# Side steps paced by the transposes' banks, the gates of the two branches apart, the conv weights loaded ahead, and the last 128 features by halves of tokens

## The chip, the core and the metric

One core of a Trainium2 chip. The metric is device time in microseconds (us) of one execution of the whole step, as the median of the runs shown. TensorE is called PE in the rows, VectorE DVE, ScalarE ACT, GpSimd POOL and SyncE SP.

## The reference

A step of a decoder trunk of two layers, all in fp32, for a prompt of 512 tokens and 8 sample tokens that share the weights. For each layer, on tokens x of 1024 features:

```python
xn = rmsnorm(x, g_mix)
u_a, v_a, q, k, v, gate_a, gate_b = split(xn @ w_in)      # 512, 512, 3 x 768, 2 x 1024 columns
a_out = gelu(u_a) * (tril(w_s) @ rmsnorm(gelu(v_a), g_v) + b_s)   # chunks of 128 tokens, 8 groups
b_out = merge of 3 dilated window attentions over q, k, v  # QK norm, rotary, softmax; 12 heads of 64
merged = sigmoid(gate_a) * (a_out @ w_a_proj) + sigmoid(gate_b) * (b_out @ w_b_proj)
x = x + merged @ w_o
up = rmsnorm(x, g_ffn) @ w_up                              # 2 x 2816 columns
c = conv_b + sum(conv_w[j] * up[t - 2 + j] for j in range(3))     # causal, along tokens
x = x + (silu(c_gate) * c_val) @ w_down
```

The sample tokens attend to cached keys and values, and their convolution starts from a cached state (`state_conv`). Outputs are the tokens after both layers, new key and value rows, conv rows and gating rows.

## The kernel before

Features lie on the 128 partitions, the 520 tokens along the free dimension in two halves of 260. Each weight block of 128 x 128 is split into a rounded part `hi` and a rest `lo` (ACT casts, DVE subtracts), and so are the activations; a block is then worth three products (hi x hi, hi x lo, lo x hi), for each half of the tokens: `triple` issues these six matmuls, all at line L362. Some tiles of the feed-forward use seven products in place of eight (`dense2`). PSUM has five banks for accumulation (`acc`) and three for everything else on PE (`tp`, from `tps()`): the transposes, the attention's scores and products, the gating products.

The order of the work is written out as a list of weight groups, whose raw blocks SP loads ahead in a ring of nine. `dense` runs a group: it takes the blocks, issues the triples, and hands the two banks of each 128 output features to a `unit` function, which reads them out at a raised priority. In each layer come the q, k and v columns of the three attentions with the u and v columns between, then the mix stage in the order of the string `mix`, then `w_o`, then the feed-forward with the up tiles and, piece by piece, the down projection. In `mix`, `gi` is a pair of features' worth of gate a (`gates`, 96 matmuls), `hi` one of gate b, `aj` 128 features of `a_out @ w_a_proj` (24 matmuls, read out by `gated`, L1378), `bj` 128 features of `b_out @ w_b_proj` (12 matmuls), added to `aj`'s and split for `w_o`.

Everything else is in generators ("side steps"): the attention blocks, the gating branch `a_branch`, the samples' attention `attn_samples`, the norms, `history` (the conv state's share), `conv_rows`, and `y_rows`, which transposes the last output back and stores it. They stand in lanes and are advanced by `pump`, which every triple calls. A planned clock `st["now"]` grows by 0.36 us for a triple into one bank and by 0.72 into two. A generator yields how long it wants to wait (times 1.1); a positive value says that its next step is heavy, a negative one that it is light. Heavy steps take 0.4 planned us each and may only follow one another at a distance (`GAP`). `finish` drains lanes at once: `a0` is preceded by `finish("v")` (the gating branch), `b0` by `finish("a", "s")` (attention and samples), the norm before the feed-forward by `finish("v")` (history). The order of emission gives each instruction its priority; a scheduler that runs when the program is built orders each engine's queue by it, and the engines run their queues in order.

`conv_columns` is the first part of `history` in layer 0: it brings the conv weights of both layers into columns (`cwc`), by a load of rows and a transpose for each of the three taps. In the last `into_x` of layer 1 (m = 7) 128 output features are accumulated in two banks that are filled in turn and added to `x`; `ready` counts the features that are done, and `y_rows` waits on it, for features 0 to 3, 4 to 6 and 7.

Of the kernel before, what the change touches and what calls it, by code (L numbers as in the profile page):

```python
# [22 lines left out]
H2 = 260  # L23
# [59 lines left out]
DELAY0 = 1.0  # L83
GAP = 0.7
SLACK = 1.1
# [4 lines left out]
def step_kernel(ctx: ExitStack, tc: tile.TileContext, a, o):  # L90
# [68 lines left out]

    mix = "g0 g1 g2 a0 a1 g3 a2 a3 h0 a4 a5 h1 h2 b0 a6 b1 b2 a7 b3 h3 b4 b5 b6 b7".split()  # L160
    for l in range(DEPTH):
# [65 lines left out]
    for g, grp in enumerate(groups):  # L227
# [10 lines left out]
        for k, k1 in steps(nk):  # L238
# [3 lines left out]
    raws, splits, parts4 = [], {}, {}  # L242
    st = {"raw": 0, "taken": 0, "split": 0, "used": set(), "g": 0, "now": 0.0, "last": -9.0,
          "pin": False, "limit": 0}
# [81 lines left out]
    def pump(force=()):  # L326

        while True:
            e = [q + [n] for n, k in LANES.items() if not force or n in force for q in tasks[n][:k]]
            if not force:  # L330
                e = [q for q in e if q[0] <= st["now"] and (q[2] or st["now"] >= st["last"] + GAP)]
            if not e:
                return
            due, g, light, n = min(e, key=lambda q: q[0])
            st["now"] = max(st["now"], due)
            lane = tasks[n]
            i = next(i for i, q in enumerate(lane) if q[1] is g)
            if not light:
                st["now"] += 0.4
                st["last"] = st["now"]  # L340
            try:
                d = next(g)
                lane[i][0] = st["now"] + SLACK * abs(d)
                lane[i][2] = d < 0
            except StopIteration:
                lane.pop(i)
            if force:
                return
# [262 lines left out]

    def conv_columns():
        for j in range(3):
            cr = tmp(128)
            for l in range(DEPTH):
                dma(cr[l * 44 : l * 44 + 44], a["conv_w"][l, j].rearrange("(m p) -> m p", p=128))
            yield 4.0
            t = tps()
            pe.transpose(t[:, :88], cr[:88], ident[:88, :88])
            dve.tensor_copy(cwc[:, j], t[:, :88])  # L620


# [48 lines left out]
    def y_rows():  # L671
        for k0, k1 in ((0, 4), (4, 7), (7, 8)):
# [3 lines left out]
            yield 1.3  # L676
            if n == 128:
                t = tps()
                for b in range(4):
                    pe.transpose(t[:, b * 128 : b * 128 + 128], x[:, k0, b * 128 : b * 128 + 128], ident)  # L680
                y = tmp(512).rearrange("p (b m) -> p b m", b=4)
                dve.tensor_copy(y, t.rearrange("p (b m) -> p b m", b=4))  # L682
                dma(o["yp"][0, :, k0 * 128 :].rearrange("(b p) m -> p b m", p=128), y)
            for b in range(4) if n > 128 else ():
# [12 lines left out]
            act.copy(ys[:, k0 * 128 : k1 * 128], t[:NB, :n])  # L697
        dma(o["ys"][:, 0], ys)


    for l in range(DEPTH):
# [681 lines left out]
        for g, j in mix:  # L1383
# [3 lines left out]
            elif g == "a":  # L1387
                if j == 0:
                    finish("v")
                    add("v", history())  # L1390
                gated(m1[j], As)
            else:
                if j == 0:
                    finish("a", "s")
                g = gb[j]
                gated(g, Bx)
                dve.tensor_tensor(g, g, m1[j], op=ALU.add)
                mgs.append((tmp(T, F32R), tmp(T, F32R)))
                split_f(*mgs[j], g)
# [93 lines left out]
        def down(g):  # L1493
            return [hs[k] for k in range(*pieces[g])]

        for op, i, *m in ffn:
            if op == "up":
# [10 lines left out]
        for m in (0, 2, 3, 4, 5, 6, 7):  # L1508
            into_x(m, down(3), 1.0, norm, last)
        if norm:  # L1510
# [40 lines left out]
```

## Time and profile before

| | |
|---|---|
| median of 3 runs | 1578.58 us (1576.14 to 1580.62) |
| profiled execution | 1577.19 us, of which the span from first to last instruction is 1575.2 us |
| PE busy | 1537.3 us, 98% |
| DVE busy | 1195.7 us, 76% |
| ACT busy | 781.1 us, 50% |
| POOL busy | 196.3 us, 12% |
| mean granted clock of PE | 0.994 |

A row of a group of instructions gives line, engine, operation, what is written and read, its count, and the time. Matmuls overlap in the records, so one that lasts 280 ns is followed by the next after some 120 ns; waits and stretches tell more of PE than its busy time.

### The profile page before, as it was taken

The page shows a single profiled execution, that of the slowest core. Times are in us where ns is not written, and L with a number is a line of the kernel's source. Part 1 is how long each engine was busy: PE and PEld are TensorE (multiplying, and loading weights), DVE is VectorE, ACT ScalarE, POOL GpSimd, SP SyncE. Part 2 cuts the span into 40 slices and gives each one's busy share as a digit, 9 for nine tenths or more (in the row PEclk, how much of TensorE's full clock was granted, in tenths as well). Part 3 has the DMA queues.
Part 4 walks back from the last instruction along what each step waited for, and adds up shares of the span by engine and source line. Part 5 has one row for each costly group of instructions (what it writes and reads, how often), then busy time and mean ns, then how long its engine had stood idle before and what let it go on. Part 6 is the DMA issues. An engine that isn't in the chain of part 4 may idle for free. (4 is left out here: it accounts for less than half of the span.)

```text
span 1575.2 us, 33158 instructions
## 1 busy us (share of the span) xinstructions
PE 1537.3 (98%) x12745; PEld 1508.1 (96%) x12745; DVE 1195.7 (76%) x2507; ACT 781.1 (50%) x1676; POOL 196.3 (12%) x138
## 2 busy tenths in 40 slices
PE   7999999999999999899999999999999999999998
PEld 7999899999999999899999998999999999999998
DVE  5677868866588898888848686878566979988793
ACT  6564535434354554555545554553344555545452
POOL 1112010000000132133002030100000003322210
PEclk9999999999999999999999999999999999999999
DMA  7443333533322323332444333334332223342331
GB/s 208 139 119 114 96 114 95 163 88 109 88 74 80 109 85 105 91 98 87 115 120 127 100 123 88 111 106 149 93 103 84 72 85 101 91 117 78 98 89 66
DMA packets 298301, 164.38 MB, mean 104 GB/s; under 512 B 18599, under 2 KB 291767, under 8 KB 298127
## 3 DMA queue, kind: packets, MB, share of 16 engines
q1 hardware_dynamic: 298143, 162.26, 35.3%
q8 instruction: 101, 1.65, 0.4%
q14 instruction: 57, 0.47, 0.1%
HBM read 154.66 MB, written 10.36 MB: 105 GB/s over the span
## 5 line engine op out<-in xcount | busy, mean ns | idle before, releaser
L362 PE MATMUL acc<-t,whi 128*128 128x260 f32 x7584 | 1306.1, 286 | 18.2 <-ACT t L465 7.6
L362 PEld LDWEIGHTS acc<-t,whi 128*128 128x128 f32 x7584 | 1094.7, 189 | 26.7 <-ACT t L465 9.2
L362 PE MATMUL acc<-t,wlo 128*128 128x260 f32 x3792 | 880.0, 285 | 0.0
L362 PEld LDWEIGHTS acc<-t,wlo 128*128 128x128 f32 x3792 | 633.9, 189 | 2.4 <-issue 0.7
L298 ACT CAST whi<-raw 128x512 fp32r<-128x512 f32 (+2 forms) x518 | 299.1, 579 | 481.8 <-PE acc L362 348.1
L299 DVE TENSOR_TENSOR wlo<-raw,whi 128x512 fp32r<-128x512 f32 (+2 forms) x518 | 351.7, 680 | 119.8 <-ACT whi L298 116.3
L1432 DVE SCALAR_TENSOR_TENSOR t<-t,cwc,t 128x510 f32<-128x510 f32 (+1 forms) x176 | 146.1, 841 | 22.0 <-ACT t L1430 21.8
L281 POOL TENSOR_TENSOR sum<-raw,raw 128x512 f32<-128x512 f32 x40 | 61.3, 1532 | 485.2 <-DMA raw<-in_w_up_dram 328.7
L138 POOL TENSOR_TENSOR rr<-ss,mhalf 128x8 f32<-128x8 f32 (+1 forms) x30 | 56.2, 1872 | 287.9 <-DVE ss L801 212.7
L1124 DVE TENSOR_TENSOR t<-acc,t 128x260 f32<-128x260 f32 x144 | 54.7, 419 | 34.9 <-PE acc L362 34.9
L298 ACT CAST whi<-sum 128x512 fp32r<-128x512 f32 x80 | 49.6, 620 | 61.2 <-PE acc L362 61.1
L609 ACT CAST t<-t 128x520 fp32r<-128x520 f32 (+1 forms) x84 | 47.2, 563 | 54.7 <-DVE t L1449 31.6
L1407 DVE TENSOR_TENSOR x<-acc,x 128x260 f32<-128x260 f32 x128 | 48.8, 419 | 31.8 <-PE acc L362 31.1
L1430 ACT ACTIVATE t<-t,vcol,cwc 128x520 f32<-128x520 f32 x88 | 72.1, 820 | 0.0
L299 DVE TENSOR_TENSOR wlo<-sum,whi 128x512 fp32r<-128x512 f32 x80 | 58.7, 737 | 16.8 <-ACT whi L298 16.6
L610 DVE TENSOR_TENSOR t<-t,t 128x520 fp32r<-128x520 f32 (+1 forms) x84 | 53.9, 644 | 12.5 <-ACT t L609 11.2
L138 POOL TENSOR_TENSOR rc<-ms,mhalf 128x5 f32<-128x5 f32 x4 | 4.7, 1177 | 430.9 <-DVE ms L515 430.9
L457 DVE TENSOR_TENSOR t<-acc,t 128x260 f32<-128x260 f32 x100 | 41.6, 423 | 7.4 <-PE acc L362 5.4
L911 ACT ACTIVATE t<-t,stat 128x128 f32<-128x128 f32 (+1 forms) x96 | 40.0, 419 | 7.7 <-DVE stat L908 7.3
L1189 DVE TENSOR_TENSOR t<-acc,t 128x260 f32<-128x260 f32 x76 | 29.2, 421 | 16.8 <-PE acc L362 14.9
L1448 ACT ACTIVATE t<-t 128x520 f32<-128x520 f32 x44 | 28.0, 637 | 24.1 <-DVE t L1432 15.1
L281 POOL TENSOR_TENSOR sum<-sum,raw 128x512 f32<-128x512 f32 x20 | 32.7, 1635 | 19.9 <-issue 19.0
(202 smaller groups left out, 1259.1 us busy)
## 6 DMA issues: line engine op xcount, KB each, us to landing
raw<-in_w_up_dram SPq DMA_DIRECT2D x176, 256.0 KB
raw<-in_w_in_dram SPq DMA_DIRECT2D x162, 256.0 KB
raw<-in_w_down_dram SPq DMA_DIRECT2D x96, 192.0 KB
t<-in_cache_kv_w_dram SPq DMA_DIRECT2D x48, 256.0 KB
raw<-in_w_o_dram SPq DMA_DIRECT2D x32, 256.0 KB
raw<-in_w_a_proj_dram SPq DMA_DIRECT2D x16, 256.0 KB
raw<-in_w_down_dram SPq DMA_DIRECT2D x32, 128.0 KB
out_dram<-t SPq DMA_DIRECT2D x15, 256.0 KB
```

What stands on the lines that cost most here:

```text
L138: pool.tensor_tensor(out, in_, mhalf[: in_.shape[0], :n], op=ALU.pow)
L281: pool.tensor_tensor(s, p, q, op=op)
L298: kept(act.copy(hi[:, :nk], r))
L299: kept(dve.tensor_tensor(lo[:, :nk], r, hi[:, :nk].bitcast(F32), op=ALU.subtract))
L362: mm = pe.matmul(b, wi, xi[:, h * H2 : h * H2 + H2], start=start and i == 0, stop=stop and i == 2,)
L457: return lambda acc: dve.tensor_tensor(out, acc, p, op=ALU.add)
L609: act.copy(hi, src)
L610: dve.tensor_tensor(lo, src, hi.bitcast(F32), op=ALU.subtract)
L1124: dve.tensor_tensor(v2(g)[:, h], acc, n.rb[:, h], op=ALU.mult)
L1407: dve.tensor_tensor(xm, acc, xm, op=ALU.add)
L1430: act.activation(cv, up, AF.Identity, scale=cwc[:, 2, i : i + 1], bias=vcol[:, 32 + i : 33 + i])
L1432: dve.scalar_tensor_tensor(cv[:, s:TP], up[:, : TP - s], cwc[:, j, i : i + 1], cv[:, s:TP], op0=ALU.mult, op1=ALU.add)
```

## The change

Four edits. `pump` no longer asks for a distance between heavy steps; it holds three slots, each taken by a heavy step for 3.0 planned us, and lets a heavy step go when one is free. In `mix` all groups of gate a and the `a` stand ahead of those of gate b and the `b`, except that `b0` to `b2` begin among the `h`; `history` is added after `a7` instead of before `a0`. `conv_columns` issues its six loads in a first step, waits 8.0, and then transposes the three in steps of their own. The last 128 features of the last layer are accumulated one half of the tokens after the other (`last_rows`), each added to `x` when it is done; `y_rows` transposes and stores each half by itself, the first by ACT, the second by DVE; and the sample rows' store is issued by ACT's queue instead of SP's.

```diff
--- before.py
+++ after.py
@@ -81,7 +81,7 @@
 
 SEVEN = tuple(("up", i) for i in (9,10,12,13,15,16,18,19,20,21))
 DELAY0 = 1.0
-GAP = 0.7
+BUSY = 3.0
 SLACK = 1.1
 URGENT = 60
 
@@ -157,7 +157,7 @@
             if 0 <= i - i0 < 3:
                 ffn.extend(("down", g, sum(ns[: i - i0]) + j) for j in range(ns[i - i0]))
 
-    mix = "g0 g1 g2 a0 a1 g3 a2 a3 h0 a4 a5 h1 h2 b0 a6 b1 b2 a7 b3 h3 b4 b5 b6 b7".split()
+    mix = "g0 g1 a0 a1 g2 a2 a3 g3 a4 a5 a6 a7 h0 h1 b0 h2 b1 b2 h3 b3 b4 b5 b6 b7".split()
     for l in range(DEPTH):
         w_in = a["w_in"][l]
 
@@ -240,7 +240,7 @@
                 loads.append((w, k0 + k, k1 - k, c))
                 blocks.append((g, (k, c)))
     raws, splits, parts4 = [], {}, {}
-    st = {"raw": 0, "taken": 0, "split": 0, "used": set(), "g": 0, "now": 0.0, "last": -9.0,
+    st = {"raw": 0, "taken": 0, "split": 0, "used": set(), "g": 0, "now": 0.0, "free": [0.0] * 3,
           "pin": False, "limit": 0}
     at = {b: i for i, b in enumerate(blocks)}
 
@@ -328,7 +328,7 @@
         while True:
             e = [q + [n] for n, k in LANES.items() if not force or n in force for q in tasks[n][:k]]
             if not force:
-                e = [q for q in e if q[0] <= st["now"] and (q[2] or st["now"] >= st["last"] + GAP)]
+                e = [q for q in e if q[0] <= st["now"] and (q[2] or st["now"] >= min(st["free"]))]
             if not e:
                 return
             due, g, light, n = min(e, key=lambda q: q[0])
@@ -337,7 +337,8 @@
             i = next(i for i, q in enumerate(lane) if q[1] is g)
             if not light:
                 st["now"] += 0.4
-                st["last"] = st["now"]
+                st["free"].remove(min(st["free"]))
+                st["free"].append(st["now"] + BUSY)
             try:
                 d = next(g)
                 lane[i][0] = st["now"] + SLACK * abs(d)
@@ -610,14 +611,16 @@
         dve.tensor_tensor(lo, src, hi.bitcast(F32), op=ALU.subtract)
 
     def conv_columns():
+        rows = [tmp(128) for _ in range(3)]
         for j in range(3):
-            cr = tmp(128)
             for l in range(DEPTH):
-                dma(cr[l * 44 : l * 44 + 44], a["conv_w"][l, j].rearrange("(m p) -> m p", p=128))
-            yield 4.0
+                dma(rows[j][l * 44 : l * 44 + 44], a["conv_w"][l, j].rearrange("(m p) -> m p", p=128))
+        yield 8.0
+        for j in range(3):
             t = tps()
-            pe.transpose(t[:, :88], cr[:88], ident[:88, :88])
+            pe.transpose(t[:, :88], rows[j][:88], ident[:88, :88])
             dve.tensor_copy(cwc[:, j], t[:, :88])
+            yield 1.0
 
 
     x = cp.tile([128, 8, T], F32, name="x")
@@ -674,13 +677,19 @@
             while ready[0] < k1:
                 yield -0.7
             yield 1.3
-            if n == 128:
+            for h in range(2) if n == 128 else ():
+                while ready[0] < k1 + h:
+                    yield -0.5
                 t = tps()
-                for b in range(4):
-                    pe.transpose(t[:, b * 128 : b * 128 + 128], x[:, k0, b * 128 : b * 128 + 128], ident)
-                y = tmp(512).rearrange("p (b m) -> p b m", b=4)
-                dve.tensor_copy(y, t.rearrange("p (b m) -> p b m", b=4))
-                dma(o["yp"][0, :, k0 * 128 :].rearrange("(b p) m -> p b m", p=128), y)
+                for b in range(2):
+                    c = h * 256 + b * 128
+                    pe.transpose(t[:, b * 128 : b * 128 + 128], x[:, k0, c : c + 128], ident)
+                y = tmp(256).rearrange("p (b m) -> p b m", b=2)
+                with urgent():
+                    (act.copy if h == 0 else dve.tensor_copy)(y, t[:, :256].rearrange("p (b m) -> p b m", b=2))
+                dma(
+                    o["yp"][0, h * 256 : h * 256 + 256, k0 * 128 :].rearrange("(b p) m -> p b m", p=128), y
+                )
             for b in range(4) if n > 128 else ():
                 t = tps()
                 for k in range(k0, k1):
@@ -695,7 +704,7 @@
                 j = (k - k0) * 128
                 pe.transpose(t[:NB, j : j + 128], x[:, k, TP:], ident)
             act.copy(ys[:, k0 * 128 : k1 * 128], t[:NB, :n])
-        dma(o["ys"][:, 0], ys)
+        act.dma_start(o["ys"][:, 0], ys)
 
 
     for l in range(DEPTH):
@@ -1387,8 +1396,9 @@
             elif g == "a":
                 if j == 0:
                     finish("v")
+                gated(m1[j], As)
+                if j == 7:
                     add("v", history())
-                gated(m1[j], As)
             else:
                 if j == 0:
                     finish("a", "s")
@@ -1493,6 +1503,23 @@
         def down(g):
             return [hs[k] for k in range(*pieces[g])]
 
+        def last_rows(xs):
+
+            g = st["g"]
+            st["g"] += 1
+            _, _, _, nk, (c,) = groups[g]
+            held = [(k0, k1, block(g, (k0, c))) for k0, k1 in steps(nk)]
+            for h in range(2):
+                acc = acc_tile()
+                for k0, k1, (hi, lo) in held:
+                    for k in range(k0, k1):
+                        xk = [t[:, h * H2 : h * H2 + H2] for t in xs[k]]
+                        triple((hi[:, k - k0], lo[:, k - k0]), xk, [acc], k == 0, k == nk - 1)
+                xm = v2(x[:, 7])[:, h]
+                with urgent():
+                    dve.tensor_tensor(xm, acc, xm, op=ALU.add)
+                ready[0] += 1
+
         for op, i, *m in ffn:
             if op == "up":
                 h_tile(i)
@@ -1506,7 +1533,10 @@
         else:
             norm = Norm(l * 8 + 8)
         for m in (0, 2, 3, 4, 5, 6, 7):
-            into_x(m, down(3), 1.0, norm, last)
+            if last and m == 7:
+                last_rows(down(3))
+            else:
+                into_x(m, down(3), 1.0, norm, last)
         if norm:
             norm.finish()
         finish("v", "s")
```

## Rows read from the trace of the kernel before

**Rows 1.** The page, engines: busy us, share of the span, instructions.
```profile
PE 1537.3 (98%) x12745; PEld 1508.1 (96%) x12745; DVE 1195.7 (76%) x2507; ACT 781.1 (50%) x1676; POOL 196.3 (12%) x138
```

**Rows 2.** Waits of PE: us in total, times, longest us.
```profile
PE tp L619 <- DMA t<-in_conv_w_dram: 2.3, 1, 2.3
PE acc L362 <- DVE t L1378: 2.1, 1, 2.1
...
PE tp L926 <- ACT t L928: 1.9, 2, 1.0
```

**Rows 3.** Timeline, layer 0: start us, us, engine, line, operation.
```profile
289.17 0.80 SPq L616 DMA_DIRECT2D t<-in_conv_w_dram  x2
...
293.27 0.38 PE L619 MATMUL tp<-cst,t 88*128 88x88 f32 x1 [2.33 <-DMA t<-in_conv_w_dram]
```

**Rows 4.** Windows after two waits: from:to, us, engines busy, clock, DMA share, GB/s.
```profile
293.25:296.65 3.40, 3.38 (x16) 3.40 (x17) 3.40 (x10) 0.61 (x2) 0.00 (x0) 0.50 0.97 291
296.65:300.00 3.35, 3.35 (x31) 3.35 (x31) 3.35 (x10) 1.40 (x5) 0.00 (x0) 1.00 1.02 322
...
1068.05:1071.47 3.42, 3.42 (x18) 3.42 (x17) 3.42 (x11) 1.85 (x4) 0.00 (x0) 0.50 1.01 339
1071.47:1076.00 4.53, 4.53 (x40) 4.53 (x39) 4.53 (x13) 1.42 (x3) 0.00 (x0) 1.00 0.62 197
```

**Rows 5.** Windows of the transposes' clusters (PE, PEld, DVE, ACT, POOL; clock).
```profile
188.27:193.34 5.07, 3.22 (x31) 2.03 (x30) 3.84 (x10) 3.50 (x14) 0.00 (x0) 1.00 0.23 48
193.34:200.00 6.66, 6.66 (x56) 6.66 (x57) 3.30 (x8) 2.88 (x8) 0.00 (x0) 1.00 0.32 81
...
960.70:965.65 4.95, 3.09 (x30) 1.95 (x29) 3.46 (x10) 3.51 (x14) 0.00 (x0) 1.00 0.17 46
965.65:969.10 3.45, 3.45 (x19) 3.40 (x16) 1.33 (x4) 1.48 (x5) 0.00 (x0) 0.51 0.08 5
969.10:975.00 5.90, 5.90 (x52) 5.90 (x51) 2.51 (x4) 1.41 (x4) 0.00 (x0) 1.00 0.31 89
```

**Rows 6.** Line 1108, the samples' last transposes: ns min/median/max, first and last start.
```profile
L1108 PE MATMUL tp<-cst,t x8: 170/256/256, 327.5 to 1100.6; 128*128 128x8 f32 x8
```

**Rows 7.** Timeline, layer 0, DVE: the gating branch's last product.
```profile
190.26 0.69 DVE L1307 SCALAR_TENSOR_TENSOR t<-t,t 128x520 f32<-128x520 f32 x1
```

**Rows 8.** Windows of the cache burst in both layers (third column DVE).
```profile
289.00:299.60 10.60, 8.27 (x59) 8.06 (x58) 10.60 (x31) 2.39 (x6) 0.00 (x0) 0.84 1.01 318
...
1063.70:1073.60 9.90, 7.85 (x55) 7.68 (x54) 9.90 (x29) 2.86 (x6) 0.00 (x0) 0.83 1.00 327
```

**Rows 9.** Groups of DVE from 289 to 317: count, busy us, mean ns, idle before.
```profile
L299 DVE TENSOR_TENSOR wlo<-raw,whi 128x512 fp32r<-128x512 f32 x8 | 5.4, 681 | 0.0
...
L1378 DVE SCALAR_TENSOR_TENSOR t<-t,acc 128x260 f32<-128x260 f32 x6 | 2.4, 416 | 0.3 <-PE acc L362 0.3
...
L1335 DVE TENSOR_TENSOR t<-t,cwc 128x176 f32<-128x176 f32 x4 | 1.2, 330 | 0.0
...
L1341 DVE TENSOR_TENSOR hc<-t 128x176 f32<-128x176 f32 x2 | 0.7, 330 | 0.0
```

**Rows 10.** Timeline of the end.
```profile
1569.06 0.41 PE L362 MATMUL acc<-t,wlo 128*128 128x260 f32 x2
...
1569.38 0.76 DVE L1407 TENSOR_TENSOR x<-acc,x 128x260 f32<-128x260 f32 x2 [4.56 <-PE acc L362]
...
1570.67 0.69 DVE L682 COPY t<-tp 128x512 f32<-128x512 f32 x1 [0.53 <-PE tp L680]
1571.06 0.30 SPq L698 DMA_DIRECT2D out_dram<-ys  x1
1571.77 0.38 SPq L683 DMA_DIRECT2D out_dram<-t  x1
```

**Rows 11.** Window of the last store's data (last columns DMA share, GB/s).
```profile
1572.50:1573.75 1.25, 0.00 (x0) 0.00 (x0) 0.00 (x0) 0.00 (x0) 0.00 (x0) 0.79 0.68 216
```

**Rows 12.** Waits of SP's queue: us in total, times, longest us.
```profile
SPq L265 <- DVE wlo L299: 777.1, 349, 8.1
```

## The prediction

> **What bounds the kernel now.** I read the engine totals first. TensorE (PE) is busy 1537.3 of 1575.2 us, VectorE (DVE) 76% [rows 1], so PE is the bound and only what stops or slows PE can be won: at most some 38 us of idle time and what the clock costs. Next the waits of PE, longest total first [rows 2]. Three kinds lie in stages that the diff touches: one wait of 2.3 us for the load of the conv weights, one of 2.1 us for DVE's `gated` (L1378), and short ones of the attention's transposes on ScalarE (ACT) copies.
>
> The timeline shows the first: the third pair of conv loads is issued at 289.17, in the middle of a burst of cache loads, and the transpose of L619 that needs it starts at 293.27 after 2.33 us of waiting [rows 3]. PE runs its queue in order, so the accumulations behind it stand too. The windows show the second half of the price: after that wait the granted clock is 0.50 (1.2 instead of 2.4 GHz) from 293.25 to 296.65, and 16 PE instructions take 3.40 us where the next stretch does 31 in 3.35 [rows 4]. The same happens in layer 1 after the wait for `gated`: 18 instructions in 3.42 us, then 40 in 4.53. Without transposes between, an accumulation matmul costs 6.66 / 56 = 0.119 us [rows 5]; I use it as PE's price.
>
> **The change, part by part.**
>
> *Conv weights.* Six loads before the first transpose instead of two before each: no work is added but one more `yield`. The first transpose is due 8 x 1.1 = 8.8 us after the issues. The loads need three times 0.80 us of SP issue plus gaps, some 3 us, and the last pair took 4.1 us from issue to its use, in a stretch of saturated DMA [rows 3]; 7.1 is less than 8.8. They also move from ahead of `a0` to behind `a7`, past the cache burst. Gain: 2.33 us of wait and 3.40 - 16 x 3.35 / 31 = 1.67 us of half clock, **4.0 us**. Bounds: 0 (the loads come late again) to 4.0; I take 4.0, for the one thing that was late has 1.7 us to spare. Six issues in a row on SP hold raw loads up by some 3 us; the raw ring runs five blocks of 2.9 us ahead, which hides it. The three tiles held instead of one come out of 61. Next late after this wait are the outputs of `gated` in the full DVE of that stretch, below. POOL's queue is passed by nothing.
>
> *Order of the mix stage.* The same groups in another order. Counting 48 matmuls to a feature of a gate, 24 to an `a`, the groups ahead of `b0` are 816 matmuls before and 768 after, so `b0` comes 48 x 0.119 = 5.7 us earlier. `b0` forces the attention and the samples to their end; the samples' last transposes run at 327.5 in layer 0 and `b0` stood, by count, at 340.6 [rows 6], so some 7 us of margin stay and this costs nothing; with the margin gone it would cost the excess. `a0` comes 11.5 us earlier; the gating branch that it waits for ran its last L1307 at 190.26 in layer 0 [rows 7], long before either place, so nothing there.
>
> The place to watch is the cache burst. From 289.0 to 299.6 DVE is busy 10.60 of 10.60 us and in layer 1 from 1063.7 to 1073.6 9.90 of 9.90 [rows 8]: it adds up the sampled V rows. There PE waited for `gated`. In the new order `a4` to `a7`, four in a row, lie about there. Their DVE work is 8 x 0.416 for the outputs and 4 x 0.68 for the weights, 6.0 us in 11.4; two features' worth of gate `h0` takes 4 x 0.416 + 4 x 0.68 = 4.4 [rows 9]. So 1.6 us more DVE where it is full; `history` leaving the same stretch takes away 1.2 us of L1335 and some 0.7 of the add behind it. About even. But five accumulation banks, two to an output, leave 1.5 outputs of slack, which is 4.3 us with `a` and 8.6 us with gates. The old wait with its half clock cost 2.05 + 3.42 - 18 x 4.53 / 40 = 3.4 us [rows 2, 4]. Bounds: -3.4 (gone) to +3.4 (one more like it); DVE's load is nearest to the old one with an earlier finish of `history`, so I take half of the gain, **1.7 us**.
>
> *Pacing.* Before, a heavy step follows another after 0.4 + 0.7 = 1.1 planned us, so four span 3.3. After, three may come at once and the fourth 3.4 after the first. The mean rate hardly moves (0.91 to 0.88 per us); what moves is the bunching, and with it the whole order of the attention's transposes. What that order loses now: from 188.27 to 193.34 31 PE instructions take 5.07 us against 3.7 at 0.119, 1.4 us; layer 1 repeats it from 960.70 (30 in 4.95, 1.4) and loses 3.45 - 19 x 5.90 / 52 = 1.3 to the clock behind it [rows 5]; two waits of L926 on an ACT copy add 1.9 [rows 2]. Together 6.0. Bounds: all of it gone, -6.0, or as much again, +6.0. Three steps now meet three banks, but in the old order too the fourth met the first one's bank at nearly the same distance, so I take little: **1.0 us**.
>
> *The end.* The last accumulation ends at 1569.47. Then two adds (to 1570.14), four transposes, a copy of 512 columns (0.69), and the store issued at 1571.77, 0.41 after the copy because the store of `ys` had gone out on SP at 1571.06 [rows 10]. After: one add of half the tokens (to 1569.92), two transposes (to 1570.34), a copy of 256 columns (0.42, as an add of 260), and SP free of `ys`: issue at some 1570.85, 0.9 us earlier. The first half's add, transposes and copy run under the second half's 18 matmuls (2.1 us); the copy is on ACT, and behind ACT's wait and issue stands only `ys`. The matmuls are as many as before. The store's data took 1.25 us [rows 11]; half of it 0.6. **1.5 us**; bounds 0 (the `ys` store or the first half ends last) to 1.9.
>
> Here a rule speaks against the change. The Trainium skill, "DMA: Bandwidth & Descriptors", Rules for kernel authors, says of two transfers to disjoint partition halves not to bother, as they share the same engines and serialize. (Here the halves are of tokens and each spans all 128 partitions.) By it the 0.6 us would not come, and this part would be 0.9 and the sum 0.6 smaller. I keep 0.6, since the first half's store is over before the second's begins.
>
> Sum: 4.0 + 1.7 + 1.0 + 1.5 = 8.2 us off the profiled execution's 1577.19 (span 1575.2 and 2.0 around it): 1569.0. That execution stands 1.4 below the median of the runs, 1578.58, which the prediction is for: **1570.4**.
>
> **Rivals.**
>
> *The attention's clusters dissolve too.* Three steps to three banks let ACT and DVE empty each bank before it is asked for again. For it: the waits of L926 are for copies out of banks [rows 2]. Against: the cluster at 188.27 waits for exponentials, not for a bank. 4.0 + 3.4 + 6.0 + 1.5 = 14.9 off: 1563.7. Chance 0.15.
>
> *No change.* The conv wait goes and a new one of the `gated` kind takes its place in one layer: -4.0 - 1.5 + 3.4 = -2.1: 1576.5. For it: DVE is full there and order is all that decides. Or the change does not do what it says: raw loads ahead of the six on SP have waited up to 8.1 us for a slot [rows 12], more than the 1.7 to spare, and PE waits for the conv weights again: -4.2, 1574.4. Chance 0.25 for both.
>
> *Slower.* One mechanism: `a4` to `a7` against the full DVE. PE stops when an output's two reads come over 4.3 us late; each stop costs 3.4 with its half clock. From -5.5 (conv and end) it takes three to be measurably slower; two in each layer give +8.1: 1586.7. For it: `gated` was the very output that stopped PE before, and four now follow each other. Against: in layer 0 the same stretch held without a stop for DVE, and `history` leaves. Chance 0.15.
>
> **How the numbers follow.** The forecast as summed has 0.45; its own range is 1566 to 1574. A measurement of this kernel tells no difference within about 0.3%, 4.7 us: faster is below 1573.8, slower above 1583.3. Faster: 0.43 of the forecast and the 0.15 of dissolving, 0.58. Same: the no-change cases and the upper edge of the forecast, 0.27. Slower: 0.15. The range for 8 in 10 runs from the dissolving case to short of the slower one: 1563 to 1581.
>
> **What would show it.** PE waits: no L619 for `in_conv_w` over 0.5 us, and the granted clock 1.0 near 290. `gated` (L1378 before): PE's wait for it below 1 us in both layers. L1330's transposes after the last `a`, in the `h` groups. At the end: last store's issue about 1.4 us after the last accumulation's end instead of 2.3, with 128 KB. Waits of L926 and L936: about as much as before. Wrong it would be with new half-clock stretches in the mix stage, or with the clusters of qkv and uv gone altogether.

## The result, and the profile of the changed kernel

| | before | changed |
|---|---|---|
| median of 4 runs on one chip | 1578.39 us (1576.14 to 1580.62) | 1559.99 us (1558.54 to 1561.80) |
| profiled execution, its span | 1577.19, 1575.2 | 1560.41, 1558.6 |
| mean granted clock of PE | 0.994 | 0.998 |

The ratio is 0.9887, interval 0.9874 to 0.9901: 18.4 us faster, beyond the lower end of the range. The direction was right, the size less than half of what came.

The page of the changed kernel, engines, answers to [rows 1]:

```profile
PE 1527.1 (98%) x12745; PEld 1500.0 (96%) x12745; DVE 1195.7 (77%) x2507; ACT 777.0 (50%) x1677; POOL 196.6 (13%) x138
```

The same 12745 PE instructions: the span fell by 16.6 and PE's *busy* time by 10.2 of them. So most of the gain is not idle time that went; it sat inside what the profile counts as busy.

The waits of PE in the changed kernel (total us, times, longest):

```profile
PE acc L363 <- DVE t L1198: 4.5, 3, 1.7
...
PE tp L945 <- ACT t L937: 1.9, 2, 1.6
PE acc L363 <- DVE t L1387: 1.9, 2, 1.1
...
PE tp L935 <- ACT t L937: 1.0, 2, 0.5
PE tp L897 <- DVE t L911: 0.9, 2, 0.5
```

The wait for the conv weights of [rows 2] is gone. `gated` (L1387 now) still stops PE once in each layer, by 1.1 and 0.8. The attention's waits for ACT (L935 and L945 now, L926 and L936 before) were forecast to stay as they were. Before, there were 1.9 in [rows 2] and two lines more,

```profile
PE tp L926 <- ACT t L911: 2.0, 2, 1.0
...
PE tp L936 <- ACT t L928: 1.4, 2, 0.7
```

5.3 in all; now it is 2.9. So this list shows only a small part of the gain.

The stage table does. Stages are bounded by counting accumulation matmuls in the trace (288 for a group of q, k and v, 192 for one of u and v, 1056 for a mix stage); both layers together, us. "All else" begins with the first accumulation, some 10 us into the span. "Listed waits" and "half clock" are those of the attention's and the mix stages alone (qkv and uv without the very first, and mix).

| | attention's qkv and uv | mix | first qkv | all else | listed waits | stretches at half clock |
|---|---|---|---|---|---|---|
| before | 352.0 | 311.5 | 47.1 | 854.5 | 9.7 | 3 |
| changed | 342.0 | 305.5 | 46.2 | 854.9 | 5.6 | 0 |
| difference | -10.0 | -6.0 | -0.9 | +0.4 | -4.1 | |

Of the 16.0 us in the first two columns 4.1 are listed waits, and some 4.4 the three half-clock stretches (1.7, 1.4 and 1.3, as worked out from [rows 4, 5]). The other 7.5 lie in PE's busy time. The first qkv differs through the half clock at the start: it lasts 3.4 or 6.8 us in the profiled executions, with no pattern by kernel (6.8 with the slots alone, 3.4 in the changed kernel), and is not counted as the change's.

Windows of the changed kernel where [rows 4, 8] had the stops (columns as there):

```profile
291.00:296.50 5.50, 5.50 (x47) 5.38 (x46) 5.50 (x13) 1.99 (x4) 0.00 (x0) 1.00 0.91 284
296.50:300.00 3.50, 2.44 (x20) 2.23 (x20) 3.50 (x10) 1.17 (x3) 0.00 (x0) 1.00 0.32 93
1060.00:1064.00 4.00, 3.19 (x27) 2.98 (x26) 4.00 (x10) 1.22 (x3) 0.00 (x0) 1.00 0.25 74
1064.00:1068.00 4.00, 4.00 (x36) 4.00 (x35) 4.00 (x10) 0.91 (x2) 0.00 (x0) 1.00 0.22 66
```

DVE (third column) is still full, and PE loses 1.06 and 0.81 us there to `gated`, but the clock stays at 1.00.

### The profile page after: what moved, and what is told of

It reads as the page before. It is cut to its first block, busy times and chain, and to the rows that moved or that the text cites. A ratio compares the mean times of both kernels' runs of the same rounds, so it can differ in the third digit from the quotient of the medians.

```text
span 1558.6 us, 33142 instructions
## 1 busy us (share of the span) xinstructions
PE 1527.1 (98%) x12745; PEld 1500.0 (96%) x12745; DVE 1195.7 (77%) x2507; ACT 777.0 (50%) x1677; POOL 196.6 (13%) x138
## 5 line engine op out<-in xcount | busy, mean ns | idle before, releaser
L363 PE MATMUL acc<-t,wlo 128*128 128x260 f32 x3792 | 889.0, 284 | 0.0
L1442 DVE SCALAR_TENSOR_TENSOR t<-t,cwc,t 128x510 f32<-128x510 f32 (+1 forms) x176 | 147.4, 849 | 21.6 <-ACT t L1440 21.4
L138 POOL TENSOR_TENSOR rr<-ss,mhalf 128x8 f32<-128x8 f32 (+1 forms) x30 | 59.6, 1987 | 286.4 <-DVE ss L810 193.7
L1198 DVE TENSOR_TENSOR t<-acc,t 128x260 f32<-128x260 f32 x76 | 29.3, 422 | 16.6 <-PE acc L363 15.2
```

Source lines behind the costliest of these rows:

```text
L138: pool.tensor_tensor(out, in_, mhalf[: in_.shape[0], :n], op=ALU.pow)
L363: mm = pe.matmul(b, wi, xi[:, h * H2 : h * H2 + H2], start=start and i == 0, stop=stop and i == 2,)
L1442: dve.scalar_tensor_tensor(cv[:, s:TP], up[:, : TP - s], cwc[:, j, i : i + 1], cv[:, s:TP], op0=ALU.mult, op1=ALU.add)
```

## The experiments

The time of the kernel before, given with each, is from the same chip; "-" is faster. The expectations weigh a few explanations against each other: 'slots' (it helps that three heavy steps may go together), 'rate' (it helps that fewer heavy steps go to a matmul), 'new deal' (any other order may do as well or as badly) and 'parts as forecast'. A run of one kernel is profiled once, so stages and waits below are those of one execution.

**The parts alone.** First the pacing by slots with nothing else of the change.

```diff
-GAP = 0.7
+BUSY = 3.0
...
-                e = [q for q in e if q[0] <= st["now"] and (q[2] or st["now"] >= st["last"] + GAP)]
+                e = [q for q in e if q[0] <= st["now"] and (q[2] or st["now"] >= min(st["free"]))]
...
-                st["last"] = st["now"]
+                st["free"].remove(min(st["free"]))
+                st["free"].append(st["now"] + BUSY)
```

> The kernel before with the pacing alone changed (three slots of 3.0 planned us in place of the distance of 0.7). Theory 'slots': the pacing is what shortened the q, k, v and u, v stages, by 10.8 us in the two traces, so 9 to 12 us faster than before, with the conv wait and its half clock still there. Theory 'parts as forecast': about 1 us. Theory 'new deal': the order of the side steps is simply another one and all four edits deal it; then this could be anything from 5 us slower to 10 faster, and the q, k, v stages need not look like those of the changed kernel.

1562.18 against 1577.45, ratio 0.9909 (0.9897 to 0.9922): -15.3, where the prediction had 1.0, and more than any of the theories had. The attention's stages take 342.5, all but the changed kernel's; mix 306.7. Against the expectation the wait for the conv weights is gone here too, and so is the one for `gated`; PE waits 1.4 us for the conv state's load (L1331) instead.

Then the opposite, the changed kernel with the old pacing (the rule of `pump` is the old one again):

```diff
-BUSY = 3.0
+GAP = 0.7
...
```

> The changed kernel with the old pacing (distance 0.7). Theory 'slots': the mix stages give their 6.0 us and the rest nothing, so 5 to 7 us faster than before, 10 to 12 slower than the changed kernel, and the q, k, v stages have the lengths of before to 0.3 us. Theory 'parts as forecast': 7 faster than before. Theory 'new deal': the q, k, v stages differ from both.

1570.89, ratio 0.9965 (0.9953 to 0.9977): -6.6. The attention's stages take 351.9, as before; mix takes 304.8.

The order alone, with `history` behind `a7`:

```diff
-    mix = "g0 g1 g2 a0 a1 g3 a2 a3 h0 a4 a5 h1 h2 b0 a6 b1 b2 a7 b3 h3 b4 b5 b6 b7".split()
+    mix = "g0 g1 a0 a1 g2 a2 a3 g3 a4 a5 a6 a7 h0 h1 b0 h2 b1 b2 h3 b3 b4 b5 b6 b7".split()
...
-                    add("v", history())
+                if j == 7:
+                    add("v", history())
```

> The kernel before with the new order of the mix stage and history behind a7, old pacing, old conv loads, old end. If the order alone takes the conv weights' loads out of the burst of cache loads: about 6 us faster, L619 without a wait. If only loading ahead cures that wait: 2 to 3 faster, from the wait for gated in layer 1 alone.

1570.87, 0.9967 (0.9956 to 0.9979): -6.6, the same as all three other edits together, and PE does not wait for the conv weights although their loads are in the old form. So beside the order the early loads and the new end add nothing that can be measured.

The conv weights loaded ahead, alone:

```diff
+        rows = [tmp(128) for _ in range(3)]
         for j in range(3):
-            cr = tmp(128)
...
-            yield 4.0
+        yield 8.0
+        for j in range(3):
             t = tps()
...
```

> The kernel before with the six conv loads issued ahead and nothing else. Forecast's term: 4.0 us faster (2.33 of wait, 1.67 of half clock). If the burst of cache loads holds up all six just as well, or PE waits for gated instead in layer 0 as in layer 1: 0 to 1 us.

1580.86 against 1577.45, 1.0020 (1.0011 to 1.0030): +3.4, rather a loss; the profiled execution is one of the faster ones, 1578.01. Its waits of PE:

```profile
PE tp L1332 <- DMA t<-in_state_conv_dram: 3.6, 2, 2.0
PE acc L362 <- DVE t L1380: 3.5, 2, 1.9
```

The wait for `in_conv_w` went as forecast, and two others took its place: `history` now reaches its next load, the conv state, inside the same burst of cache loads, and PE waits for that; and for `gated` in both layers. What was late was whatever `history` loads in that burst.

**How often a heavy step goes.** The other series changes one number of the kernel before, the distance `GAP`. `pump` is asked only by triples. With 0.4 for the step itself, 0.7 is over after one triple (0.72), 0.9 only after two (1.44), 1.6 after three. One heavy step then goes with every 6, 12 or 18 accumulation matmuls, if steps are due.

```diff
-GAP = 0.7
+GAP = 0.5
```

> The kernel before with its distance between heavy steps cut from 0.7 to 0.5 planned us (0.9 from step to step), nothing else. Theory 'slots' (letting up to three heavy steps go together is what helps): steps still come singly, so within 4 us of before, and the q, k, v and u, v stages stay near 47.8, 29.9 and 50 us. Theory 'new deal' (any other order may do as well): the stages change as much as with the slots, in either direction, over 6 us.

1577.20 against 1578.28, 0.9993 (0.9984 to 1.0002). Every engine's instructions stand in the same order as before: the distance acts only in steps of whole triples. (Its trace serves below for the kernel before.)

```diff
-GAP = 0.7
+GAP = 0.9
```

> The same with a distance of 0.9 (1.3 from step to step). Theory 'slots': within 4 us of before. Theory 'new deal': over 6 us away from before, in either direction, and unlike the run with 0.5.

1550.51 against 1578.28, 0.9821 (0.9806 to 0.9836): -27.8, faster than the changed kernel by 9. Its timeline early in the mix stage of layer 0 (start us, us, line, what, count):

```profile
220.47 0.60 PE L845 MATMUL tp<-cst,t 128*128 128x128 f32 x4
220.82 0.72 PE L362 MATMUL acc<-t,whi 128*128 128x260 f32 x4
221.38 0.40 PE L362 MATMUL acc<-t,wlo 128*128 128x260 f32 x2
221.63 0.64 PE L362 MATMUL acc<-t,whi 128*128 128x260 f32 x4
222.10 0.41 PE L362 MATMUL acc<-t,wlo 128*128 128x260 f32 x2
222.35 0.60 PE L845 MATMUL tp<-cst,t 128*128 128x128 f32 x4
```

Between the steps stand 4 + 2 + 4 + 2 = 12 matmuls. The waits of PE in this kernel, those of the attention, the gating branch, `history` and `gated`, are down to a single one:

```profile
PE tp L926 <- ACT t L873: 1.0, 1, 1.0
```

The mix stage of layer 0, whole, in a kernel with the order of before (distance 0.5):

```profile
214.10:369.90 155.80, 153.59 (x1282) 150.14 (x1281) 120.76 (x333) 69.49 (x167) 9.07 (x9) 0.99 0.39 116
```

and with distance 0.9:

```profile
209.90:358.40 148.50, 148.50 (x1282) 145.74 (x1281) 119.73 (x333) 70.00 (x167) 10.95 (x9) 1.00 0.41 122
```

The same 1282 recorded instructions on PE, 7.3 us less: 2.2 were idle, 1.7 is the half clock behind the conv wait, and 3.4 stood in busy time.

Further off, one step for three triples:

```diff
-GAP = 0.7
+GAP = 1.6
```

> The kernel before with a distance of 1.6, nothing else: one heavy step to three triples (2.56 planned us), where 0.9 gave one to two. Theory 'rate': still fewer waits of PE for copies and loads in the q, k, v stages, which get no longer than with 0.9; but the attention is then late and b0 forces what is left of it: a stretch of transposes with waits ahead of the b groups, and in all slower than with 0.9, 1555 to 1575. Theory 'new deal': no such pattern.

1570.58 against 1578.15, 0.9956 (0.9941 to 0.9970): -7.6. The attention's qkv and uv stages get shorter still (328.3), but 130 transposes and products are left over at their end and fall into the mix stages, which take 331.1 with 20.5 us of half clock. There `b0` forces what is left, and PE waits for the samples:

```profile
PE tp L1108 <- ACT t L609: 3.5, 1, 3.5
PE tp L1108 <- DVE t L1104: 2.5, 1, 2.5
```

Between these, distances in turn:

```diff
-GAP = 0.7
+GAPS = (0.7, 0.9)
...
-                e = [q for q in e if q[0] <= st["now"] and (q[2] or st["now"] >= st["last"] + GAP)]
+                e = [q for q in e if q[0] <= st["now"] and (q[2] or st["now"] >= st["last"] + GAPS[st["n"] % len(GAPS)])]
...
+                st["n"] += 1
```

> The kernel before with a distance of 0.7 and 0.9 in turn: two heavy steps in single file to three triples, 9 matmuls to a step. Theory 'rate': on a falling line between 8 matmuls to a step (1567.6) and 12 (1550.5): 1560 to 1567. Theory 'new deal' (each order has its own waits, and the rate explains none of it): outside of that, 1550 to 1580.

1552.86 against 1576.33, 0.9850 (0.9836 to 0.9865): -23.5. That is off the line of theory 'rate' and where 'new deal' had it: the rate alone does not give the time of an order. The same with `GAPS = (0.9, 0.9, 1.6)`, one step to 14 matmuls:

> The kernel before with a distance of 0.9, 0.9 and 1.6 in turn: three heavy steps in single file to seven triples, 14 matmuls to a step. Theory 'rate': the q, k, v stages give 1 to 3 us more than with 12 matmuls; the mix stage decides: 1546 to 1552 if the attention is still through before b0, 1553 to 1565 with a forced run of transposes ahead of the b groups if it is not.

1554.88, 0.9855 (0.9839 to 0.9872): -21.4. The samples begin to be late at `b0` (2.0 us for L1109). With `GAPS = (0.7, 0.7, 0.9)`, three steps to four triples, 8 matmuls to a step, the share of the changed kernel's slots but in single file:

> The kernel before with a distance of 0.7, 0.7 and 0.9 in turn: heavy steps in single file, three to four triples, which is the mean rate of three slots of 3.0 without their bunching. Theory 'rate alone': as the slots of 3.0 alone, 1558 to 1566. Theory 'both' (the slots at the old rate gave 5.7 of 15.3 us, so bunching has that share): 1566 to 1571.

1567.58 against 1576.88, 0.9936 (0.9916 to 0.9956): -9.3.

**How many go at once.** In slots of 3.0, three steps go together. They take 1.2 planned us and the first slot is free 3.4 after the first step. Triples come at 1.92, 2.64, 3.36 and 4.08: the third misses by 0.04, so it takes four triples, 8 matmuls to a step. Slots of 2.9 are free at 3.3, after three triples: the old 6 matmuls, in threes.

```diff
-BUSY = 3.0
+BUSY = 2.9
```

(`BUSY` here and in the next three on the pacing alone.)

> The kernel before with the slots alone, taken for 2.9 in place of 3.0 planned us. The pacing is asked only at a triple, 0.72 planned us and six matmuls apart, so the distance of 0.7 gave one heavy step to a triple; three slots of 3.0 give three steps to four triples, and 2.9, just short of it, three to three triples: the old rate, in threes. Theory 'rate' (fewer heavy steps to a matmul is what helps): the gain over before is gone, 1573 to 1583. Theory 'slots' (threes meet three banks): like 3.0, 1559 to 1565.

1572.48 against 1578.15, 0.9970 (0.9959 to 0.9981): -5.7. `BUSY = 2.0`:

> The kernel before with the slots alone, each taken for 2.0 in place of 3.0 planned us: steps may come in threes and the mean rate rises from 0.88 to 1.25 per us. Theory 'slots': bunching stays, so most of the 15 us stays, 8 to 16 faster than before, less what PE waits for banks that are not yet empty. Theory 'new deal': as likely slower as faster than the kernel with 3.0 by 5 us or more.

1587.29 against 1578.28, 1.0053 (1.0036 to 1.0070): +9.0, with the first slot free 2.4 after the first step, two triples, 4 matmuls to a step. Its longest waits of the transposes:

```profile
PE tp L927 <- ACT t L912: 6.3, 9, 1.2
...
PE tp L937 <- ACT t L929: 2.9, 2, 1.7
PE tp L889 <- DVE t L903: 2.9, 6, 0.8
```

`BUSY = 4.0`, 10 matmuls to a step:

> The same with 4.0: threes, at 0.68 per us. Theory 'slots': 10 to 16 faster than before, with fewer waits of PE for banks; unless the attention is late at b0 and steps are forced there, which would show as a run of transposes without matmuls ahead of the b groups. Theory 'new deal': anywhere from 1555 to 1582.

1566.80 against 1578.28, 0.9919 (0.9903 to 0.9936): -11.5. `BUSY = 5.0`, 12 matmuls to a step:

> The kernel before with slots alone, of 5.0: three heavy steps to six triples, the mean rate of the distance of 0.9, in threes. Theory 'rate alone': as that one, 1548 to 1554. Theory 'threes cost at a low rate' (4.0 was no better than 3.0): 1560 to 1568.

0.9875 (0.9858 to 0.9891), -19.7, between the two theories: four runs of 1554.8 to 1558.0. A fifth, the profiled execution, took 3807 us and was as slow in every stage; it is left out, so this kernel has no profile to read.

All of them together, in us against before:

| matmuls to a heavy step | in single file | three at once |
|---|---|---|
| 4 | | +9.0 (2.0) |
| 6 | 0 (before), -1.1 (0.5) | -5.7 (2.9) |
| 8 | -9.3 | **-15.3** (3.0, the change) |
| 9, 10 | -23.5 (9) | -11.5 (10) |
| 12 | **-27.8** (0.9) | -19.7 (5.0) |
| 14 | -21.4 | |
| 18 | -7.6 | |

The share of steps is the trend. Three at once is some 6 us better at 6 and 8 matmuls, and 8 worse at 12. Single orders lie several us off any smooth line (9 and 10).

Where the time sits can be worked out from the same traces. The attention's and the mix stages have 4320 accumulation matmuls and 1128 small instructions (transposes, products) in every kernel. In the table "small" is the time from the start of each small instruction, or of the matmul just before one, to the next start, and "matmuls" the same from matmul to matmul; waits, and half of the time at half clock, are taken out of both and stand by themselves (us).

| kernel | matmuls to a step | small | matmuls | waits | lost to half clock |
|---|---|---|---|---|---|
| slots of 2.0 | 4, threes | 132.6 | 511.8 | 20.0 | 5.1 |
| before | 6 | 138.0 | 510.8 | 9.7 | 5.1 |
| slots of 2.9 | 6, threes | 137.3 | 511.8 | 10.1 | 0 |
| slots of 3.0 | 8, threes | 130.3 | 511.8 | 7.1 | 0 |
| 0.7, 0.7, 0.9 | 8 | 128.1 | 511.8 | 11.8 | 3.4 |
| 0.7, 0.9 | 9 | 125.0 | 511.4 | 3.3 | 0 |
| slots of 4.0 | 10, threes | 134.4 | 510.8 | 4.0 | 5.1 |
| 0.9 | 12 | 128.4 | 509.9 | 1.0 | 1.7 |
| 1.6 | 18 | 128.4 | 511.7 | 9.1 | 10.2 |

In single file the small instructions cost 138 at 6 matmuls to a step and 125 to 128 from 8 on; more room than that no longer helps them, and the gain of 0.9 over 0.7, 0.7, 0.9 is waits and clock. Slots of 2.9 gain nothing there, but have no half clock in these stages: what threes gave at the old rate is the clock. Slots of 2.0 and 4.0 fit no line by rate.

**Together.** The changed kernel's other edits with the distance of 0.9 and the old rule:

```diff
-BUSY = 3.0
+GAP = 0.9
...
```

> The changed kernel with its slots taken out and the old rule with a distance of 0.9 in their place. Theory 'rate': as good as or better than the kernel before with 0.9 (1550.5), the order of the mix stage adding at most 2 us as it did on top of the slots: 1547 to 1552, 8 to 13 below the changed kernel. If the slots have a share of their own that a single file lacks: 1553 or more.

1556.69 against 1578.15, 0.9863 (0.9841 to 0.9885): -21.5, 6 us worse than the distance by itself, against theory 'rate'; that the slots have a share which single file lacks, the other branch, does not follow, for the kernel before does better in single file. PE waits for the conv weights again, 1.6 us for L620, and mix takes 300.7 instead of 298.0, 2.7 of the 6; the rest stands in the first qkv and the feed-forward, where one profiled execution cannot settle whose it is. The kernel before with `GAP = 0.9` is the best version of all.

**The end.** In the changed kernel the first half's transposes were to run under the second half's matmuls. To have them emitted there:

```diff
...
+                stored.append(h)
...
+                while not h and not stored:
+                    pump(("s",))
```

> The changed kernel, with the steps of y_rows driven on behind the first half of the last 128 features until that half is stored, so that its transposes stand among the second half's matmuls. Theory 'not overlapped' (the end gained nothing because both halves' transposes and stores came after the last matmul): the last store is issued 0.5 to 1.0 us sooner after the last accumulation than in the changed kernel, where it was 2.0 us after it. Theory 'shared issue' (the last store's issue of 0.9 us, beside ACT's issue of the sample rows, is what ate the gain): its issue still takes 0.9 us and the end moves by under 0.5.

1560.36, 0.9891 (0.9872 to 0.9909), like the changed kernel; the instructions of every engine came out in the same order, so the overlap was not tested. (That all banks of `tps` were taken is the likely reason, and was not shown.) It is one more execution of the same order, though: here SP issued the two stores in 0.94 us, the second in 0.45, where the changed kernel took 1.38, and the end came no sooner (5.75 us behind the last matmul). With accumulation banks for these transposes the order did change:

```diff
...
-                t = tps()
+                t = acc_tile()
...
+                stored.append(h)
...
+                while not h and not stored:
+                    pump(("s",))
```

> The changed kernel, with y_rows driven on behind the first half of the last features and its transposes of both halves in free accumulation banks: in PE's order the first half's two transposes stand ahead of the second half's 18 matmuls. Theory 'not overlapped': the first half's store is issued under those matmuls, 1 us or more before the last of them ends, and the last store's issue takes 0.4 us and ends 0.5 to 1.0 us sooner after the last matmul than in the changed kernel; PE may stand some 0.5 us for the first half's add ahead of the transposes. Theory 'shared issue': the issue still takes 0.9.

And the changed kernel with the sample rows' store back on SP:

```diff
-        act.dma_start(o["ys"][:, 0], ys)
+        dma(o["ys"][:, 0], ys)
```

> The changed kernel with the store of the sample rows back on SP. Theory 'shared issue': SP's issue of the second half's store takes 0.4 instead of 0.9 us, and with the sample rows ahead of or behind it the end comes within 0.3 us of the changed kernel's. If ACT's queue was a gain, the last store of the three is issued 0.4 us later than in the changed kernel.

One run each: 1560.07 and 1561.64. With `ys` on SP the second store's issue took 0.45, as 'shared issue' had it; but so it did with ACT's issue beside it in the two other runs, so ACT's issue is not what made it 0.89. The timeline of the end in the changed kernel, for [rows 10]:

```profile
1552.72 0.28 PE L363 MATMUL acc<-t,wlo 128*128 128x260 f32 x1
...
1553.04 0.43 DVE L1520 TENSOR_TENSOR x<-acc,x 128x260 f32<-128x260 f32 x1 [2.28 <-PE acc L363]
...
1553.37 0.48 ACT L699 COPY t<-tp 128x384 f32<-128x384 f32 x1 [1.57 <-PE tp L697]
...
1553.50 0.84 PE L686 MATMUL tp<-cst,x 128*128 128x128 f32 x4
...
1554.12 0.36 ACT L689 COPY t<-tp 128x256 f32<-128x256 f32 x1
...
1554.38 0.42 DVE L689 COPY t<-tp 128x256 f32<-128x256 f32 x1 [0.90 <-PE tp L686]
1554.50 1.38 SPq L690 DMA_DIRECT2D out_dram<-t  x2
...
1554.86 0.59 ACTq L707 DMA_DIRECT2D out_dram<-ys  x1
```

All four transposes of L686 stand behind the last matmul, and the first half's copy on ACT stands behind ACT's copy of an earlier piece (L699). The two stores begin 1.5 and 2.0 us after the last matmul's end at 1553.00; the forecast was 1.4, before it was 2.3. With the accumulation banks the first half's transposes do come ahead of the second half's matmuls:

```profile
1550.08 0.44 PE L686 MATMUL acc<-cst,x 128*128 128x128 f32 x2
...
1553.04 0.48 ACT L700 COPY t<-tp 128x384 f32<-128x384 f32 x1 [1.99 <-PE tp L698]
...
1553.41 0.38 ACT L689 COPY t<-acc 128x256 f32<-128x256 f32 x1
...
1553.99 0.93 SPq L690 DMA_DIRECT2D out_dram<-t  x2
```

but the copy, 3 us later, again stands behind the earlier piece's in ACT's in-order queue. From the end of the last matmul to the end of the span it is 5.7 us before, 5.6 in the changed kernel, 5.6 with the banks (1552.67 to 1558.3), and 5.8 with `ys` on SP (1553.75 to 1559.5). The same stretch is 6.0 in the changed kernel with the old pacing (1563.26 to 1569.2) and in the kernel before with 0.9 (1543.92 to 1549.9), whose ends are coded as in the changed kernel and as before, so differences of 0.1 or 0.2 tell nothing.

## Why the prediction was wrong

**Pacing: the step that failed.** "The mean rate hardly moves (0.91 to 0.88 per us); what moves is the bunching." Said to be worth 1.0, measured -15.3 alone. The planned times were right and the place where they are looked at was left out: slots are asked for only at triples, so the fourth step goes not 3.4 but 4.08 planned us after the first, and a step comes with 8 matmuls instead of 6. The run with slots of 2.9, where the rate really does not move, gives -5.7; the remaining 9.6 is the rate, and single file at the same share gives -9.3. Between slots of 2.9 and of 3.0 the small instructions lose 7.0 us of busy time and the waits 3.0 (table above). The bound of 6.0 failed too: it added up listed waits and one loss of clock. It did not see the time in which PE counts as busy and its instructions merely stand further apart: from a transpose or attention product to the next instruction, or from a matmul to a transpose, the starts take 144.9 us in all before and 130.4 in the changed kernel (stages as in the table but for layer 1's first qkv, 1105 such instructions in both), and only 5.9 of these 14.5 are listed waits; from matmul to matmul, where nearly all of the half clock falls, they take 481.3 and 479.8. One stage shows it without any wait or half clock: the second qkv stage of layer 0, 288 matmuls and 100 others in each, in the order of before (distance 0.5),

```profile
86.00:133.80 47.80, 47.80 (x391) 44.66 (x390) 31.09 (x67) 27.30 (x82) 3.64 (x5) 1.00 0.34 99
```

in the changed kernel,

```profile
84.50:130.90 46.40, 46.40 (x390) 43.78 (x389) 31.58 (x68) 27.25 (x82) 3.09 (x6) 1.00 0.37 105
```

and with distances 0.7 and 0.9 in turn:

```profile
84.10:129.40 45.30, 45.30 (x390) 43.09 (x390) 31.32 (x67) 26.65 (x82) 2.71 (x5) 1.00 0.37 104
```

PE is "100% busy" in all three, and 2.5 us apart. (With 0.9 the stage has 12 small instructions more and takes 47.7, so only these three compare.) Why small steps cost less from 8 matmuls on (a bank that is emptied in time, or a copy's latency that more matmuls cover) was only argued, and why threes help at 8 and hurt at 12 stays open.

**Conv weights and order.** The wait and its half clock went, 4.0 as priced, but not by the edit that the price stood under: alone it gives no gain, and the order with `history` behind `a7` cures the wait without it, as the slots alone do. "They also move ... past the cache burst" was the working half of that step. The prediction did say that something would be late next; it named `gated`, which came, but not the conv state's load, which came as well where `history` had not moved. The mix stages fell by 6.0; the two terms had 4.0 + 1.7. On top of the pacing the order is worth only 2.2 (1562.18 to 1559.99), as the slots had removed most of the same waits.

**`gated` and the slower rival.** Half of the gain was taken, 1.7, and by the waits and the clock 1.6 came (with the slots alone `gated` stops PE nowhere, so it is not the order's alone). Layer 1 waits 0.81 instead of 2.05 and keeps its clock, layer 0 has a new wait of 1.06: the "below 1 us in both" failed by little. `a4` to `a7` in a row did not stop PE twice; that rival, and no change, are out. `b0` and `a0` cost nothing, as said.

**The end.** 1.5 was forecast, 0.1 came. The first half's work was said to run under the second half's matmuls; it did not, most likely for lack of a bank, and with banks for it because ACT runs its queue in order. And the smaller store's data did not come 0.6 sooner, because of `ys`. In the changed kernel and the run with the banks the packets of `ys`, on ACT's queue, fell among those of one half, and that half's data took 1.1 us; in the run with `ys` on SP, behind both stores, the halves took 0.58 and 0.52, and the last of the store ended 1.5 us after its issue, against 2.0 before (1.04 us of data). There `ys` came last instead. So all output data ended 4.25 us after the last matmul before, 4.1 in the changed kernel, 4.0 with the banks and 4.3 with `ys` on SP. The Trainium skill, "DMA: Bandwidth & Descriptors", Rules for kernel authors, says not to bother with two transfers to disjoint partition halves, as they serialize. Here the halves are of tokens, and with `ys` out of the way their data did come one behind the other and took no less in sum than in one store. With the banks the last of the smaller stores was issued 1.8 us after the last matmul, 0.5 earlier than before, and the end came 0.1 earlier.

**The dissolving rival** (1563.7) came nearest, by luck of the number: it took the pacing for 6.0 at most. Its reason, three banks for three steps, is not the main one: single file with 12 matmuls does better than any slots.

## What to carry to other kernels

When a program plans its own pace, find the points at which the plan is consulted: a distance of 0.5 and one of 0.7 were the same kernel, 0.9 was 28 us faster. Small work interleaved into a bound engine's queue has a price that the profile books as busy time: here some 138 us at one step to 6 matmuls and 125 to 130 at most wider spacings. Compare the span of stages with equal instruction counts, not lists of waits alone. A wait cured at its own load may only pass to the next load of the same generator; move the generator out of the crowd, and sweep the pace again afterwards, since the same edits that gained 6.6 us at one pace lost 6 at another.

## What the runs showed of the hardware

- In the kernel before, a wait of PE of 2.1 and one of 2.3 us were followed by 3.4 us at half clock (1.2 instead of 2.4 GHz) [rows 2, 4]; waits of 1.1 and 0.8 in the changed kernel's windows above were not. The length of the wait alone does not decide: one of 1.7 in the feed-forward of layer 0 (L1198, before it L1189) was followed by half clock in the changed kernel, and the same one was not in the kernel before; with distances of 0.7, 0.7 and 0.9 a wait of 3.1 us for the conv state (to 292.1) left the clock at 1.00.
- SP's two stores of 128 KB took 1.38 us to issue in the changed kernel beside ACT's own issue of 0.59. They took 0.94 in another execution with every engine's instructions in the same order and ACT's issue of 0.59 beside them, 0.93 with the accumulation banks and 0.94 with `ys` on SP. So the 1.38 is not the price of ACT's issue beside them; what it was stays open.
- A store of 256 KB had its data moved in 1.04 us; one of 128 KB in 0.52 to 0.64 alone and in 1.06 to 1.11 where the 32 KB of `ys`, issued on ACT's queue, moved in the same time (changed kernel, accumulation banks, `ys` on SP).
- In one of five executions with slots of 5.0 everything took 2.4 times as long, with the granted clock at 1.00; no cause was found.
